# A decoder layer in one kernel: the first feed-forward's second products deferred and taken in chunks with seven block products

## The chip, the cores and the metric

The kernel runs on one core of one Trainium2 chip. The metric is the device time of one execution in microseconds. A core has five engines with their own instruction queues: TensorE (PE: matmuls, with weight loads shown apart as PEld), VectorE (DVE), ScalarE (ACT), GpSimd (POOL) and SyncE (SP), which here issues the transfers between DRAM and the on-chip memory SBUF. Matmuls write to PSUM, eight banks of 128 x 512 numbers in f32.

## The reference, cut to what matters

One decoder layer on x (1024 tokens, width 1024), all in f32. The two feed-forwards have a hidden width of 2816.

```python
mod = silu(cond) @ w_mod + b_mod        # nine vectors: shift, scale, gate for three sub-layers
h = modulate(rms_norm(x, ffn1_norm), sh1, sc1)
x = x + 0.5 * g1 * ((silu(h @ w_gate1) * (h @ w_up1)) @ w_down1)
h = modulate(rms_norm(x, mix_norm), sh2, sc2)
b, c, v, u = split(h @ w_in)
# group A: short gated convolution; group B: diagonal state space model (SSM) with a GLU
x = x + g2 * (concat(rms_norm(yA), rms_norm(yB)) @ w_out)
h = modulate(rms_norm(x, ffn2_norm), sh3, sc3)
x = x + 0.5 * g3 * ((silu(h @ w_gate2) * (h @ w_up2)) @ w_down2)
y = rms_norm(x, final_norm)
```

## The kernel before, in words

**Precision.** Each f32 product is made of three matmuls: every operand is split into a high and a low part (`hi` by a cast on ACT, `lo` by a subtraction on DVE), and `mm3` issues hi x hi, hi x lo and lo x hi, each 128 x 128 by 128 x 512, into one PSUM bank. Weights are split on the chip too: `Weights` loads arrays of 1 MB (`raw`), and `pump` turns them into "granules" (`w`, 128 x 1024, hi and lo), in a ring of three or four slots that come free as `ws.free()` is called.

**Layout.** x is held transposed in SBUF: eight tiles of 128 channels, each in two halves of 512 tokens (`x[k][h]`), from the start to the end. The left operands of a feed-forward (`act1`, `act3`) are eight tiles by two halves as well.

**Feed-forward.** The hidden width is cut into eleven groups of 256 (`NGRP`); `fa3` is group 3 of the first feed-forward, `fb3` of the second. A group has a first part (gate and up projections, `fa3g`, `fa3u`), an activation, and a second part (down projection, `fa3d`), which is added to x at once: 16 updates by DVE of the form x + gate * PSUM. A plain first part is 64 calls of `mm3`, a second part 32. `seven` makes a first part with seven products of 2 x 2 blocks in place of eight (Winograd's form): 56 calls, and in return sums and differences of blocks. Of the weights these are made by GpSimd in `combine` and `split_done` (`sums`, `raw`), of the activations by `combos` on DVE (S1 to S4), of the results by DVE between products. `SEVEN_FROM` = (6, 1): the first feed-forward has six plain groups and five of seven products, the second one and ten.

In the first feed-forward each group's second part follows its first part (`down_both`, `down2`; the last two are joined in `down`). In the second, groups 1 to 8 are handled otherwise: `seven` is given `kept`, so each group's activations and their block sums (seven left operands of 512 KB) are split and stored to DRAM; after group 10 `down7` takes two chunks of four groups (`fbd0`, `fbd1`), loads the left operands again (`fetch`) and makes the second parts with seven products, 112 calls of `mm3` a chunk; products 1, 3 and 5 add up in one PSUM bank, so each waits for the addition that has read it.

**Order.** The engines run in the order in which a scheduler at compile time puts the program; what the program sets is the priority. `mm3` ends with `clock.tick()`. `Clock` keeps a list of side work (generators), and every `period` ticks it takes one step of the first one. The side work of the first feed-forward is `side1`: `ssm_base` (small tables of the SSM), then for each of eight batches `ssm_batch` (matrices `cl`, `bl`, `rot` on DVE, small matmuls `kp`, `tp` on PE, stores to DRAM) with three `mod_block` each: vectors of `mod`, each one a product and sum over a 128 x 1024 tile of w_mod (`mod_vector`, in the trace the custom operation `wm`). `clock.period` is 2.75 in first parts and 8 in second parts of groups 1 to 4; before group 5 what is left of `side1` is issued at once, and `combos` follows with period 4. The gate g1 is made in the prologue, beside group 0's last products (`gate1`, eight `wm`), since group 0's second part needs it. `after1` starts the next norm's sum of squares once the last second part of a tile is added, and `norm_into` makes the mixer's left operand from it, 8 ticks, 7 ticks and one tick a tile later.

Pools that matter: `movs["A"]` (20 tiles of 4 KB a partition: left operands, `keep`), `movs["B"]` (12), `tmp` (6 tiles of 2 KB, `t2k`), six PSUM banks (`mm_ps`) for products.

Of the kernel before, what the change touches and what calls it, by code (L numbers as in the profile page):

```python
# [21 lines left out]
P = 128  # L22
# [12 lines left out]
SEVEN_FROM = (6, 1)  # L35

CHUNKS = (0, 2)
# [5 lines left out]
PAD = 96, 88  # L43
# [185 lines left out]
def hymba_layer(ctx: ExitStack, tc, x_d, wm1_d, wmod_d, gu1_d, gs1_d, wd1_d, win_d, wout_d, glu_d, gu2_d, gs2_d, wd2_d, ds2_d, cols_d, cond_d, lam_d, bc_d, out_d):  # L229
# [13 lines left out]
    xp = pool("xp", side="right")  # L243
# [41 lines left out]
    def stream(gu, gs, wd, ds, m):  # L285


        joined = m == 1
        first = NGRP - 2 - 4 * (0 if ds is None else ds.shape[0])
        for g in range(m):  # L290
            plain([gu[2 * g], gu[2 * g + 1]])
            if g < first and not (joined and g == m - 1):
                plain([wd[g]])
        for g in range(m, NGRP):
            j = len(srcs)
            inner = m - joined < g <= first
            srcs.extend([gs[g - m, 0], wd[g - 1], gs[g - m, 1]] if inner else [gs[g - m, 0], gs[g - m, 1]])
# [6 lines left out]
        for c in range(0 if ds is None else ds.shape[0]):  # L304
# [4 lines left out]
        j, n = len(srcs), wd.shape[0]  # L309
        srcs.extend([wd[n - 2], wd[n - 1]])  # L310
        granules.extend([(i, 2 * q), (i, 2 * q + 1)] for q in range(2) for i in (j, j + 1))

    stream(gu1_d, gs1_d, wd1_d, None, SEVEN_FROM[0])
    plain([win_d[i] for i in range(8)] + [glu_d] + [wout_d[i] for i in range(4)])
    stream(gu2_d, gs2_d, wd2_d, ds2_d, SEVEN_FROM[1])
# [3 lines left out]
    xt = [[xp.tile([P, 2, HALF], F32, tag=f"x{k}_{h}", name=f"x{k}_{h}") for h in range(2)] for k in range(KT // 2)]  # L319
    x = [[xt[k // 2][h][:, k % 2, :] for h in range(2)] for k in range(KT)]  # L320
    clock = Clock(4)

# [128 lines left out]
    def mod_fetch():  # L451
        if later:
            n, b = later.pop(0)
            pool_ = (raw1, raw2)[len(later) % 2]
            r = pool_.tile([P, 2, 1024], F32, tag="raw", name=f"wm{n}_{b}")
            SP.dma_start(r[:], wmod_d[n - 2, b])
            fetched.append((n, b, r))

    def mod_block():
        n, b, r = fetched.pop(0)  # L460
        s = sb.tile([P, 2], F32, tag="ms", name=f"ms{n}_{b}", bufs=2)
        for i in range(2):
            mod_vector(r[:, i, :], s[:, i : i + 1])
            yield
        mod_done(n, 2 * b, 2 * b + 2, s[:])
        mod_fetch()


    def gu_evac(fi, h, pg, pu, a_tiles, name):
# [3 lines left out]
        a_tiles[fi, h] = split_act(af[:], name + "a")  # L473

# [30 lines left out]
    def combos(act, name, homes, engine=None):  # L505
# [6 lines left out]
        G_ = engine or V  # L512
# [11 lines left out]
        while "free" not in blocks:  # L524
            yield
        for k in range(4):
            f12, s2 = whole(a12[k], f"f12_{k}", G_), whole(blocks["S2"][k], f"s2_{k}", G_)
            yield
            G_.tensor_tensor(out=f12[:], in0=f12[:], in1=s2[:], op=ALU.subtract)
            blocks["S4"].append(split_act(f12[:], f"{name}S4_{k}", homes[3]))  # L530
# [4 lines left out]
    def seven(name, between, place=1, kept=None, then=None):  # L535
# [3 lines left out]

        def keep(left, src):  # L540
            t = mov(f"{name}{left}")
            A.copy(t[:, 0, :], src[:])
            V.tensor_tensor(out=t[:, 1, :], in0=src[:], in1=t[:, 0, :].bitcast(F32), op=ALU.subtract)
            SP.dma_start(kept[left][:], t[:].bitcast(F32))

        def minus(dst, a, b):
            V.tensor_tensor(out=dst[:], in0=a[:], in1=b[:], op=ALU.subtract)
# [1037 lines left out]
```

## Time and profile before

| | |
|---|---|
| median of 3 runs | 1755.64 us (1754.24 to 1756.39) |
| profiled execution | 1754.16 us, its span 1752.0 us |
| TensorE clock granted, mean | 0.994 |
| busy: TensorE, VectorE, ScalarE, GpSimd | 1697.6, 1241.8, 527.9, 272.1 us |
| DMA | 227.96 MB, mean 130 GB/s |
| prologue and group 0 of the first feed-forward | to 86 us |
| rest of the first feed-forward | 86 to 755 us |
| mixer | 755 to 1084 us |
| second feed-forward | 1084 to 1752 us |

The profile is of one execution. Its span goes from the first to the last instruction. In its rows, L105 is the line of the helper that records most operations, so groups are told apart by the names of their tiles: out<-in, with buffer numbers left out. A row of the timeline gives start, duration, engine, line, operation, tiles and count, and in brackets the idle time of the engine before it and what ended that. A row of a stretch gives its length, then busy time and number of instructions of PE, PEld, DVE, ACT and POOL, then the granted clock, the DMA engines' busy share and the rate in GB/s.

### The profile page before, as it was taken

The page shows a single profiled execution, that of the slowest core. Times are in us where ns is not written, and L with a number is a line of the kernel's source. Part 1 is how long each engine was busy: PE and PEld are TensorE (multiplying, and loading weights), DVE is VectorE, ACT ScalarE, POOL GpSimd, SP SyncE. Part 2 cuts the span into 40 slices and gives each one's busy share as a digit, 9 for nine tenths or more (in the row PEclk, how much of TensorE's full clock was granted, in tenths as well). Part 3 has the DMA queues.
Part 4 walks back from the last instruction along what each step waited for, and adds up shares of the span by engine and source line. Part 5 has one row for each costly group of instructions (what it writes and reads, how often), then busy time and mean ns, then how long its engine had stood idle before and what let it go on. Part 6 is the DMA issues. An engine that isn't in the chain of part 4 may idle for free.

```text
span 1752.0 us, 20474 instructions
## 1 busy us (share of the span) xinstructions
PE 1697.6 (97%) x7676; PEld 1400.3 (80%) x7676; DVE 1241.8 (71%) x2249; ACT 527.9 (30%) x838; POOL 272.1 (16%) x193
## 2 busy tenths in 40 slices
PE   4999999999999999999899999999999999999996
PEld 3787888888888888878788888878888888888886
DVE  7999998985766555573566746987777667677656
ACT  4211212122223223242212523433344443322221
POOL 0000000001112122110000021023222323323311
PEclk9999999999999999999999999999999999999998
DMA  7533556521111112214664110013344334659312
GB/s 313 218 90 130 209 189 226 195 102 39 37 60 49 48 49 72 91 50 131 198 195 130 45 52 25 24 71 146 144 161 174 147 133 157 247 232 370 110 49 96
DMA packets 76020, 227.96 MB, mean 130 GB/s; under 512 B 16273, under 2 KB 31889, under 8 KB 61202
## 3 DMA queue, kind: packets, MB, share of 16 engines
q1 hardware_dynamic: 75922, 226.66, 36.6%
q8 instruction: 60, 0.98, 0.2%
q14 instruction: 38, 0.31, 0.1%
HBM read 172.10 MB, written 50.33 MB: 127 GB/s over the span
## 4 chain that ended last, share of the span: by engine, by line
PE 84%; DVE 10%; DMA 3%; ACT 1%; issue 1%; SPq 0%; POOL 0%; DVEq 0%; ACTq 0%; POOLq 0%
PE wo L105 5%; DVE w L105 2%; PE fb10d L105 2%; PE p L105 2%; PE u L105 2%; PE fa10d L105 2%; PE fbd_1B L105 2%; PE fbd_0B L105 2%; PE b L105 1%; DMA swz<-si 1%; PE fa4u L105 1%; PE fa3g L105 1%; PE fa2u L105 1%; PE fa3d L105 1%; PE fbd_1A L105 1%; PE fb0g L105 1%
## 5 line engine op out<-in xcount | busy, mean ns | idle before, releaser
L105 ACT CAST w<-raw 128x512 fp32r<-128x512 f32 (+1 forms) x310 | 220.7, 734 | 565.8 <-issue 78.4
L105 DVE TENSOR_TENSOR w<-raw,w 128x512 fp32r<-128x512 f32 (+1 forms) x310 | 276.3, 906 | 135.6 <-ACT w L105 133.9
L161 POOL TENSOR_TENSOR sums<-raw 128x512 f32<-128x512 f32 x38 | 53.3, 1403 | 546.8 <-PE fa5u L105 409.8
L170 POOL TENSOR_TENSOR raw<-sums,raw 128x512 f32<-128x512 f32 x38 | 57.0, 1500 | 377.8 <-DVE w L105 377.3
L172 POOL TENSOR_TENSOR raw<-raw 128x512 f32<-128x512 f32 x38 | 58.6, 1543 | 111.1 <-DVE w L105 111.1
L162 POOL TENSOR_TENSOR raw<-raw 128x512 f32<-128x512 f32 x38 | 58.5, 1540 | 3.0
L105 DVE CUSTOM_DVE_ANT_0 wm<-wm,cact 128x1024 f32<-128x1024 f32 x48 | 57.9, 1212 | 0.0
L105 PE MATMUL p<-h,w 128*128 128x512 f32 x192 | 49.3, 419 | 8.3 <-DVE h L105 5.4
L105 PEld LDWEIGHTS p<-h,w 128*128 128x128 f32 x192 | 38.9, 204 | 18.5 <-DVE h L105 6.7
L361 POOL TENSOR_TENSOR n3aq<-n3aq,n3aq 128x512 f32<-128x512 f32 x5 | 6.4, 1290 | 274.1 <-ACT n3aq L105 273.9
L105 DVE TENSOR_TENSOR w<-sums,w 128x512 fp32r<-128x512 f32 x38 | 46.9, 1242 | 1.2 <-ACT w L105 0.8
L105 PE MATMUL v<-h,w 128*128 128x512 f32 x192 | 46.9, 395 | 0.0
L105 PE MATMUL c<-h,w 128*128 128x512 f32 x192 | 46.6, 394 | 0.0
L105 PE MATMUL wo<-oa,w 128*128 128x512 f32 x192 | 45.4, 391 | 0.6 <-DVE w L105 0.6
L105 PE MATMUL u<-h,w 128*128 128x512 f32 x192 | 44.8, 392 | 0.8 <-DVE w L105 0.8
L105 PE MATMUL b<-h,w 128*128 128x512 f32 x192 | 45.6, 393 | 0.0
L105 PE MATMUL wo<-ob,w 128*128 128x512 f32 x192 | 45.2, 391 | 0.0
L105 PEld LDWEIGHTS u<-h,w 128*128 128x128 f32 x192 | 35.6, 188 | 9.1 <-DVE w L105 1.2
L105 PEld LDWEIGHTS wo<-oa,w 128*128 128x128 f32 x192 | 35.8, 188 | 8.7 <-DVE w L105 1.0
L105 PEld LDWEIGHTS wo<-ob,w 128*128 128x128 f32 x192 | 35.8, 188 | 7.4
L105 PEld LDWEIGHTS b<-h,w 128*128 128x128 f32 x192 | 35.5, 188 | 7.2
L105 PEld LDWEIGHTS c<-h,w 128*128 128x128 f32 x192 | 35.4, 188 | 7.0
(1361 smaller groups left out, 4004.8 us busy)
## 6 DMA issues: line engine op xcount, KB each, us to landing
raw<-in_gs SPq DMA_DIRECT2D x30, 1024.0 KB, 4.9
wm<-in_wmod SPq DMA_DIRECT2D x24, 1024.0 KB, 5.7
raw<-in_gu SPq DMA_DIRECT2D x14, 1024.0 KB, 5.6
raw<-in_wd SPq DMA_DIRECT2D x14, 1024.0 KB, 4.8
mw<-in_wm SPq DMA_DIRECT2D x8, 1024.0 KB, 12.5
raw<-in_win SPq DMA_DIRECT2D x8, 1024.0 KB, 5.8
raw<-in_ds SPq DMA_DIRECT2D x8, 1024.0 KB, 6.2
x<-in_x SPq DMA_DIRECT2D x8, 512.0 KB, 8.2
```

Of the source, the lines that this page charges most:

```text
L105: r = getattr(self.engine, name)(*args, **kw)
L161: self.G.tensor_tensor(out=f, in0=r[2], in1=r[1], op=ALU.subtract)
L162: self.G.tensor_tensor(out=r[1], in0=r[1], in1=r[0], op=ALU.subtract)
L170: self.G.tensor_tensor(out=r, in0=s["t3"], in1=r, op=ALU.add)
L172: self.G.tensor_tensor(out=r, in0=r, in1=s["t2"], op=ALU.subtract)
L361: nc.gpsimd.tensor_tensor(out=a, in0=a, in1=sq[:, :n], op=ALU.add)
```

## The change

- `SEVEN_FROM` becomes (4, 1): in the first feed-forward groups 4 to 10 are made with seven products.
- Second parts of the first feed-forward: groups 1 to 8 keep seven left operands each in DRAM and are made by `down7` in two chunks after group 10, as in the second feed-forward. Groups 0, 9 and 10 keep their four activations in DRAM too, and their second parts are joined in `last_parts`, which goes over the two halves of the output channels and within them over the two halves of the tokens.
- The plain groups get `gu_keep` in place of `gu_evac`: activations and their block sums are split and stored.
- x is given up after group 0's left operands are made (`xp_open.close()`), and its SBUF goes to other pools; before group 9 it is loaded again.
- Side work: g1 moves out of the prologue into the first SSM batches (`gate1`); `combos` runs between `ssm_base` and the batches; S4 is made by `combos_last`, put first in the list of side work at the last plain group; the other `mod` vectors become `side2`, a vector a step, from group 9 on. Periods: 4 in groups 1 to 3, 6.5 in groups 4 to 8, 6 from group 9 on (also beyond the first feed-forward).
- The ring of weight slots has three from group 1 on (`ring1` retired); `movs["B"]` opens before group 1.
- `combos_last` is used in the second feed-forward too, without the wait for group 0.

```diff
-SEVEN_FROM = (6, 1)
+SEVEN_FROM = (4, 1)
-CHUNKS = (0, 2)
+CHUNKS = 2
+LAST = ((0, NGRP - 2, NGRP - 1), (NGRP - 2, NGRP - 1))
...
+    def mod_tile(home):
+        n, d, r = fetched.popleft()
+        dst = (mods, scl, gate)[n % 3][:, n // 3]
+        mod_vector(r, dst[:, d : d + 1])
+        if d == KT - 1:
+            mod_done(n, 0, KT, dst)
+        mod_fetch(home)
...
+    def keep(kept, left, src, name):
+        if left in kept:
+            t = mov(f"{name}{left}")
+            A.copy(t[:, 0, :], src[:])
+            V.tensor_tensor(out=t[:, 1, :], in0=src[:], in1=t[:, 0, :].bitcast(F32), op=ALU.subtract)
+            SP.dma_start(kept[left][:], t[:].bitcast(F32))
+    def keep_sums(kept, a11, a21, a22, name):
+        V.tensor_tensor(out=a22[:], in0=a21[:], in1=a22[:], op=ALU.add)
+        keep(kept, "S1", a22, name)
+        V.tensor_tensor(out=a21[:], in0=a11[:], in1=a21[:], op=ALU.subtract)
+        keep(kept, "S3", a21, name)
+        V.tensor_tensor(out=a22[:], in0=a22[:], in1=a11[:], op=ALU.subtract)
+        keep(kept, "S2", a22, name)
+    def keep_last(kept, a12, s2, name):
+        V.tensor_tensor(out=a12[:], in0=a12[:], in1=s2[:], op=ALU.subtract)
+        keep(kept, "S4", a12, name)
+    def gu_keep(fi, h, pg, pu, afs, kept, name):
+        t = t2k(f"{name}{fi}_{h}")
+        A.activation(t[:], pg[:], AF.Silu)
+        V.tensor_tensor(out=t[:], in0=t[:], in1=pu[:], op=ALU.mult)
+        keep(kept, f"A{h + 1}{fi + 1}", t, name)
+        afs[fi, h] = t
+        if len(afs) == 4 and "S1" in kept:
+            keep_sums(kept, afs[0, 0], afs[0, 1], afs[1, 1], name)
+            keep_last(kept, afs[1, 0], afs[1, 1], name)
...
-        while "free" not in blocks:
+    def combos_last(act, name, home):
+        while "S3" not in blocks or len(blocks["S3"]) < 4:
             yield
         for k in range(4):
-            f12, s2 = whole(a12[k], f"f12_{k}", G_), whole(blocks["S2"][k], f"s2_{k}", G_)
+            f12, s2 = whole(act[0][4 + k], f"f12_{k}", V), whole(blocks["S2"][k], f"s2_{k}", V)
             yield
...
     def side1():
-        mod_fetch()
-        mod_fetch()
-        with tc.tile_pool(name="sb1", bufs=1) as sb1:
+        with tc.tile_pool(name="sb1", bufs=1, side="right") as sb1:
             yield from ssm_base(sb1)
...
+        for _ in range(2):
+            mod_fetch(mod_home)
+        yield from combos(act1, "h1", "BBB")
         for b in range(NB):
             yield from ssm_batch(b)
+    def side2():
+        for _ in range(2):
+            mod_fetch(mod_mov)
+        while fetched:
+            mod_tile(mod_mov)
+            yield
...
+    clock.side.append(side1())
+    clock.period = 4
+    for g in range(1, SEVEN_FROM[0]):
+        gate_up(act1, f"fa{g}", kept[g], g == SEVEN_FROM[0] - 1)
+    clock.period = 6.5
...
+    for g in range(SEVEN_FROM[0], NGRP):
+        if g == NGRP - 2:
             while clock.side:
                 clock.step()
+            side_open.close()
...
+            open_x(ctx)
+            for h in range(2):
+                load_x(h)
+            clock.period = 6
+            clock.side.append(side2())
+        seven(f"fa{g}", lambda: None, kept=kept[g], then=(lambda n: fetch_chunk(0, n)) if g == NGRP - 1 else None)
+    down7("fad0", lefts[0], 0, lambda n: fetch_chunk(1, n))
+    down7("fad1", lefts[1], 0, fetch_last)
...
+    def last_parts():
+        for dh in range(2):
+            wd = ws.take(3)
+            for h in range(2):
+                outs = [ps(f"fald{4 * dh + i}_{h}") for i in range(4)]
+                for q, (w, a) in enumerate(zip(wd, a_last)):
+                    for fi in range(2):
+                        for i, o in enumerate(outs):
+                            mm3(o[:], w, 4 * fi + i, a[fi, h], q == fi == 0, q == 2 and fi == 1)
+                    if h:
+                        ws.free()
+                for i, o in enumerate(outs):
+                    d = 4 * dh + i
+                    V.scalar_tensor_tensor(out=x[d][h], in0=o[:], scalar=gate[:, 0, d : d + 1], in1=x[d][h], op0=ALU.mult, op1=ALU.add)
+                    after1(d, h)
```

More of the change, by code (lines that the diff above doesn't have):

```diff
@@ L1164, in hymba_layer @@
+    last_parts()
+    while clock.side:
+        clock.step()
+    es1.close()
     ring1 = ring1_open.enter_context(tc.tile_pool(name="ring1b", bufs=1, side="right"))
@@ L1444, in group0 @@
         return a_tiles
[L1446 removed]
+    clock.side.extend([combos(act3, "h3", "BAA"), combos_last(act3, "h3", "A")])
     a_prev = group0()
[L1448 to L1449 removed]
+    kept = {g: kept_for(g, g not in LAST[1]) for g in range(1, NGRP - 1)}
     HOMES = dict(A11="B", S2="A", A12="B", S3="A", S1="B", A22="A", S4="A")
[L1451 removed]
+    lefts = [{left: [] for left in HOMES} for _ in range(CHUNKS)]
     a_last = {}
[L1454 to L1457 removed]
     def fetch_last(n):
```

275 lines of the change are left out of this document (120 added, 155 removed).

## The prediction

> **What bounds the kernel now.** I read the page first (busy times, chain), then the chain in order of time, TensorE's timeline, the stretches by stage, and last the groups of VectorE (DVE).
>
> ```profile
> span 1752.0 us, 20474 instructions
> PE 1697.6 (97%) x7676; PEld 1400.3 (80%) x7676; DVE 1241.8 (71%) x2249; ACT 527.9 (30%) x838; POOL 272.1 (16%) x193
> PE 84%; DVE 10%; DMA 3%; ACT 1%; issue 1%; SPq 0%; POOL 0%; DVEq 0%; ACTq 0%; POOLq 0%
> ...
> 410.99 10.88 PE fa5g L105 x48
> 465.39 2.72 PE fa6gC L105 x12
> ...
> 91.43 7.14 PE L105 MATMUL fa0d<-fa_0a,w 128*128 128x512 f32 x30 [0.65 <-ACT fa_0a L105]
> 163.90 5.81 PE L105 MATMUL fa1d<-fa_0a,w 128*128 128x512 f32 x18 [4.13 <-DVE x L105]
> ```
>
> TensorE is the chain, and it runs at one pace: 10.88/48 and 2.72/12 both give 0.2267 us a matmul, in plain groups and in seven-product groups. In the first feed-forward from 86 us on, TensorE waits in the two places shown: 0.65 + 4.13 = 4.78 us. So time there is matmuls times 0.2267, as long as VectorE keeps up. The stretches (busy us of PE, PEld, DVE, ACT, POOL, then clock, DMA share, GB/s) show how near it is to not doing so:
>
> ```profile
> 86.00:109.00 23.00, 22.34 (x97) 17.84 (x96) 22.55 (x41) 5.02 (x8) 0.00 (x0) 1.00 0.35 105
> 109.00:182.00 73.00, 68.87 (x302) 56.25 (x302) 69.55 (x338) 14.63 (x20) 0.00 (x0) 0.98 0.32 107
> 182.00:250.00 68.00, 68.00 (x311) 55.68 (x310) 65.20 (x125) 13.10 (x18) 0.00 (x0) 1.00 0.64 224
> 552.00:612.00 60.00, 60.00 (x266) 49.67 (x266) 36.20 (x50) 16.20 (x27) 11.71 (x8) 1.00 0.15 53
> 1192.00:1230.00 38.00, 38.00 (x169) 31.45 (x169) 27.13 (x40) 15.41 (x27) 11.41 (x8) 1.00 0.41 152
> 1536.00:1574.00 38.00, 38.00 (x170) 31.45 (x169) 26.37 (x31) 9.90 (x18) 13.13 (x8) 1.00 0.58 234
> ...
> 1130.00:1140.00 10.00, 9.00 (x38) 6.60 (x37) 10.00 (x17) 5.75 (x10) 0.00 (x0) 1.00 0.06 8
> 1140.00:1150.00 10.00, 9.24 (x38) 7.04 (x39) 10.00 (x17) 2.34 (x4) 4.98 (x2) 1.00 0.24 97
> 1150.00:1160.00 10.00, 10.00 (x46) 8.26 (x45) 10.00 (x17) 1.82 (x4) 2.29 (x1) 1.00 0.01 2
> ```
>
> In 182 to 250 VectorE is 96% busy beside plain groups with side work, and TensorE loses nothing. In 1192 to 1230 a seven-product group with its stores to DRAM leaves VectorE 11 us free. Only where VectorE is full (30 of 30 us from 1130 to 1160, side work beside a seven-product group) does TensorE lose 0.76 + 1.00 = 1.76 us.
>
> **The change, part by part.** *Matmuls.* A call of mm3 is three matmuls. First parts: before, six groups of 64 calls and five of 56, 664; after, four and seven, 648. Second parts: before 11 x 32 = 352; after two chunks of 112 and 3 x 32, 320. So 48 calls or 144 matmuls go: 144 x 0.2267 = **-32.6 us**, all on the path. The two waits shown belong to fa0d and fa1d, which no longer stand there; TensorE goes from group 0 straight to group 1, so **-4.8 us**. What is late next is VectorE's work, costed below. With no other loss the span is 1752.0 - 37.4 = 1714.6.
>
> *VectorE.* The rows it is costed from:
>
> ```profile
> L105 DVE SCALAR_TENSOR_TENSOR x<-fa7d,gate,x 128x512 f32<-128x512 f32 x16 | 12.0, 750 | 7.4 <-PE fa7d L105 7.3
> L105 DVE TENSOR_TENSOR fb1S<-fb1ut,fb1S 128x512 fp32r<-128x512 f32 x2 | 1.4, 684 | 0.0
> L105 DVE TENSOR_TENSOR w<-raw,w 128x1024 fp32r<-128x1024 f32 x43 | 52.4, 1219 | 18.5 <-ACT w L105 17.9
> L105 DVE TENSOR_TENSOR w<-sums,w 128x512 fp32r<-128x512 f32 x2 | 3.5, 1738 | 0.0
> L105 DVE CUSTOM_DVE_ANT_0 wm<-wm,cact 128x1024 f32<-128x1024 f32 x48 | 57.9, 1212 | 0.0
> L105 DVE TENSOR_TENSOR cl<-cl,clt 128x576 f32<-128x576 f32 x8 | 6.0, 750 | 0.0
> L105 DVE TENSOR_TENSOR bl<-bl,blt 128x512 f32<-128x512 f32 x8 | 5.5, 684 | 0.1
> L105 DVE TENSOR_TENSOR rot<-rot,rott 128x512 f32<-128x512 f32 x16 | 10.9, 681 | 0.1
> L105 DVE TENSOR_TENSOR bb<-prm,qr 128x64 f32<-128x64 f32 x16 | 3.4, 214 | 0.0
> ...
> 1194.79 0.69 DVE L105 TENSOR_TENSOR fb1S<-fb1ut,fb1S 128x512 fp32r<-128x512 f32 x1
> 1195.40 0.69 DVE L105 TENSOR_TENSOR fb1S<-fb1uu,fb1S 128x512 fp32r<-128x512 f32 x1
> ```
>
> In a full queue starts are 0.61 apart for 0.69 shown, so durations count at 0.88. It loses 160 - 48 = 112 updates of x (-75 us at 0.67) and gains 40 additions in down7, 24 splits, 32 differences and 20 additions in the two further seven-product groups (116 x 0.61 = +71) and 18 more weight granules (about 1.2 each, +22). As a total that is near even: some 18 us more in 32.6 us less. What matters is where it piles up, which I get from the planner: one side step every 4 calls in groups 1 to 3, 6.5 in groups 4 to 8, 6 after.
>
> Group 1 (43.5 us at pace): 16 of the 18 base steps of the SSM. All base steps are some 32 us, an estimate: VectorE's time from 86 to 182 (22.55 + 69.55) less 30 updates, 10 weights, 7 wm, 14 splits and products and three quarters of batch 0, by the rows. 28 + 4 weights (4.9) + 15 operations of keeping (9.2) + group 0's rest (2) = 44: full. Price between 0 (as in 182 to 250) and 4.78 x 43.5/96 = 2.2; I take 1. Groups 2 and 3 have 42 and 38 by the same count, no price.
>
> Groups 4 to 8: side1 has 18 + 12 + 48 yields and combos_last 8; by the end of group 3, 48 steps are gone, group 4 takes 8 or 9, so about 30 batch steps fall on three and a half groups, 8.6 a group. A batch after the gate vectors is 5 steps: three cl (2.26), three bl (2.05), six rot (4.09), six bb (1.3), two small (0.4) = 10.1, at 0.88 8.9 us, 1.78 a step. So VectorE needs 27.1 + 15.3 = 42.4 us, while TensorE needs 38.1 + 1.7 batches of kp and tp at 1.39 each (below), 40.5. That is 105%.
>
> ```profile
> 332.92 1.05 PE L105 MATMUL kp<-cl,bl 128*16 128x128 f32 x8
> 333.89 0.66 PE L105 MATMUL tp<-ident,bl 128*128 128x128 f32 x4
> 334.31 0.94 PE L105 MATMUL fa4u<-h,w 128*128 128x512 f32 x3
> ```
>
> Price: excess 1.9 x 3.5 = 6.6; or 1.76/30 of 138 us = 8.1. From below 0 (96% cost nothing in 182 to 250). I take **8.1**: the row with a seven-product group and a full VectorE is the nearest. Group 4 has S4 made late: its eight steps start 16 calls before, and the last is forced at the product that reads it: +1.
>
> Groups 9, 10 and down7: side2 has 48 vectors wm, one every 6 calls (4.08 us), 1.21 + 0.08. Groups 9 and 10 keep four left operands, not seven: 36.2 (552 to 612) less 16 updates and 2 weights, 23, + 12 = 35 of 38. Chunk 0: 26.4 + 12.1 = 38.5 of 38: full for 76 us. But there an accumulation waits for an addition that is three to four half products back (8 us), against 2.7 in a seven-product group; I take 2, between 0 and 4.5.
>
> *DMA and SP.* Added on SP's queue: 68 stores and 68 loads of 512 KB, 8 loads of x, and the vectors in 512 KB pieces. The stores wait in SP's queue for VectorE's splits, with weight loads behind them; the second feed-forward does the same 60 times and TensorE is at 38.00 of 38 there, so nothing. The loads of a chunk:
>
> ```profile
> 1530.00:1540.00 10.00, 10.00 (x46) 8.28 (x45) 9.59 (x12) 3.83 (x7) 4.86 (x4) 1.00 1.03 419
> ...
> fb1lS<-kept1S SPq DMA_DIRECT2D x4, 512.0 KB, 10.2
> wm<-in_wmod SPq DMA_DIRECT2D x24, 1024.0 KB, 5.7
> ```
>
> The queue is full there at 419 GB/s, and wm adds 128 GB/s (524288 B in 4.08 us). A product of chunk 1 is asked for when the same product of chunk 0 has ended its second pass and is read a pass later, 38.1 - 5.4 = 32.7 us, so that is covered; a wm in the middle is not (rival 3). [...]
>
> x is read again at group 9, some 90 us before its first update: nothing. The prologue loses 8 wm (they move into batches 0 to 2, inside the steps counted). At the end of the first feed-forward the first half's norm has 24 calls (16.3 us) to cover it, not 32; the only wait of u now is on a weight, so 0:
>
> ```profile
> 764.14 1.20 PE L105 MATMUL u<-h,w 128*128 128x512 f32 x4 [0.80 <-DVE w L105]
> ```
>  Period 6 stays for the second feed-forward, where combos runs at 4 now: fewer steps beside fb0d (at best its 1.76 us go), but four steps of S4 are forced at fb1 (two blocks of four operations and a cast, 2 x 5 x 0.61 = 6.1 us, less the 2.7 us of a product); +1, between -1.8 and +3.4.
>
> *Sum.* 1714.6 + 1 + 8.1 + 1 + 2 + 1 = 1727.7. The profiled execution took 1754.16, 2.16 more than its span, and the median of three runs is 1.48 above that: 1727.7 + 2.2 + 1.5 = **1731**.
>
> **The rivals.** (1) The cover holds: VectorE's work fits as in 182 to 250, and nothing is lost. 1714.6 + 3.6 = 1718. For it: the 96% of that stretch. Against: 105% in three groups.
>
> (2) VectorE against GpSimd. In 1192 to 1230 GpSimd is busy 11.41 us and the two w<-sums of VectorE take 1738 ns, not 684: it is held up, some 2.5 us a group now. 29 of the 39 operations of VectorE there read two SBUF tiles. If it is never idle, three quarters of 11.4, 8.5 us, collide: +6.0 a group, 48.4 against 40.5, 7.9 x 3.5 = 27.7 in place of 8.1: **1751**. Against: from 1130 to 1160 GpSimd ran 7.3 us beside a full VectorE and TensorE lost 1.76 in all. [...]
>
> (3) Slower: wm waits for its transfer. Two are in flight, so each has 8.16 us to land, and VectorE stands behind a wm that isn't there. Chunk loads land after 10.2. Were all 48 so late, a step takes 5.1, not 4.08: 48 x 1.0 = 49, less the 2 counted: 1778. It turns slower when the mean landing passes 9.2 us (24.2 us of gain left over 48 steps, 0.5 each). Against: the full stretches are some 70 of 196 us, and down7 has 8 us of cover.
>
> **How the numbers follow.** Forecast 0.54 (1722 to 1743), cover 0.23 (1716 to 1722), lock 0.14 (1743 to 1759), late wm 0.09 (above 1759). About 0.2% (3.5 us) is what can be told from no change: 1752.1 to 1759.2. Of the lock, 0.08 is below it, 0.06 in it. Faster 0.85, same 0.06, slower 0.09. 1717 to 1749 leaves out late wm, the upper half of the lock and the edge of the cover.
>
> **What would show it.** 7532 matmuls on TensorE; fa1g right after group 0, no fa0d before the chunks; idle of TensorE in groups 5 to 8 by DVE of about 8 us, VectorE at 95% there; the second feed-forward some 25 us earlier. Wrong if TensorE idles over 30 us there, or if VectorE idles for DMA wm.

## Result: slower by 2.2%

1794.22 us median (1793.23 to 1795.72) against 1754.94 (1753.06 to 1756.39): ratio 1.0225, 95% interval 1.0207 to 1.0243. Forecast were 1731 and, as the case on the other side, 1778.

The page of the changed kernel, its first part, the granted clock by slices, and the groups of the conversion of weights and of the vectors:

```profile
span 1792.4 us, 20836 instructions
PE 1690.4 (94%) x7532; PEld 1382.6 (77%) x7532; DVE 1307.8 (73%) x2286; ACT 569.0 (32%) x934; POOL 357.3 (20%) x241
...
PEclk9999999999999899999999999999999999999998
...
L107 ACT CAST w<-raw 128x512 fp32r<-128x512 f32 (+1 forms) x358 | 237.6, 689 | 564.3 <-POOL raw L172 139.3
L107 DVE CUSTOM_DVE_ANT_0 wm<-wm,cact 128x1024 f32<-128x1024 f32 x56 | 76.8, 1381 | 5.2 <-DMA wm<-in_wmod 5.1
```

The matmuls that were to go are gone (7532), and the span is still 40.4 us longer. All of it lies in the first feed-forward: from the end of group 0's first part to the first product of `u` it takes 710.4 us (from group 1's first product at 84.7 to 795.1), before 669.2 (from `fa0d` at 86.2 to 755.4). What follows takes 997.3 and 996.6. So the question is where in 710 us the saving went. From the starts of each stage's first product on TensorE, against the pace of the sum (0.2267 us a matmul, and 1.4 us for the `kp` and `tp` of a batch):

| stage | us | at pace | lost | allowed in the prediction |
|---|---|---|---|---|
| groups 1, 2 | 87.0 | 87.0 | 0 | 1 (with group 3) |
| group 3 | 53.8 | 46.3 | 7.5 | |
| groups 4 to 8 | 216.1 | 198.8 | 17.3 | 9.1 |
| groups 9, 10 | 80.6 | 76.2 | 4.4 | 2 (with the chunks) |
| two chunks (down7) | 205.6 | 152.3 | 53.3 | |
| last parts | 67.2 | 65.3 | 1.9 | 0 |

The view by windows (length, then busy time of PE, PEld, DVE, ACT and POOL, granted clock, DMA share and GB/s), for group 3, group 7, group 10, chunk 0, chunk 1 and the last parts:

```profile
171.80:225.60 53.80, 48.77 (x218) 39.34 (x217) 47.07 (x81) 13.97 (x23) 7.81 (x6) 0.94 0.62 196
...
353.00:401.40 48.40, 43.31 (x194) 34.53 (x192) 46.67 (x79) 17.83 (x31) 14.12 (x8) 0.96 0.46 164
...
477.40:522.30 44.90, 40.63 (x169) 32.15 (x168) 43.95 (x62) 13.72 (x24) 17.57 (x10) 0.96 0.73 252
522.30:637.90 115.60, 90.87 (x349) 68.20 (x349) 77.19 (x114) 18.95 (x34) 22.73 (x16) 0.90 0.90 337
637.90:727.90 90.00, 82.55 (x337) 64.83 (x336) 65.85 (x90) 19.21 (x33) 21.10 (x14) 0.94 0.72 265
727.90:795.10 67.20, 67.20 (x306) 55.87 (x305) 26.79 (x44) 16.69 (x23) 10.92 (x8) 1.00 0.14 48
```

In groups 7 and 10 VectorE is full (47 of 48 and 44 of 45 us), and in group 3 it is busy 47 of 54. In chunk 0 no engine is full: TensorE 79%, VectorE 67%, and only the DMA share is high (0.90, at 337 GB/s). So the two losses are of different kinds. What TensorE waits for, in the chunks and then in groups 3 to 8:

```profile
PE fad_0A L107 <- ACT w L107: 13.7, 2, 13.2
PE fad_0B L107 <- ACT w L107: 7.0, 4, 3.6
PE fad_0A L107 <- DVE w L107: 3.6, 2, 1.9
PE fad_0C L107 <- DMA fa1lS<-kept1S: 3.3, 2, 2.4
...
PE kp L107 <- DVE bl L107: 11.9, 5, 5.0
PE fa4gC L107 <- DVE fa4gt L107: 2.5, 1, 2.5
PE fa5gC L107 <- DVE fa5gt L107: 1.9, 1, 1.9
PE fa4gC L107 <- DVE h1S L107: 1.7, 1, 1.7
```

In the chunks it is the *weights* that are late, and most at one place, the second pass of chunk 0 (a chunk goes over its seven products twice, each pass for half of the output channels). The timeline there, of SyncE's queue (start, length of the run of issues, transfer, count), then VectorE, ScalarE and TensorE:

```profile
553.94 0.32 SPq L107 DMA_DIRECT2D kept10A<-fa10A  x1
...
565.72 0.32 SPq L107 DMA_DIRECT2D kept10A<-fa10A  x1
...
568.34 12.37 SPq L107 DMA_DIRECT2D wm<-in_wmod  x6
580.80 0.38 SPq L107 DMA_DIRECT2D raw<-in_ds  x1
582.26 0.33 SPq L107 DMA_DIRECT2D wm<-in_wmod  x1
582.68 1.11 SPq L107 DMA_DIRECT2D raw<-in_ds  x1
...
552.02 1.29 DVE L107 TENSOR_TENSOR w<-raw,w 128x512 fp32r<-128x512 f32 x2 [2.39 <-ACT w L107]
...
576.70 0.69 DVE L107 TENSOR_TENSOR fad_0u<-fad_0u,fad_0C 128x512 f32<-128x512 f32 x1 [4.44 <-PE fad_0C L107]
...
577.98 1.22 DVE L107 CUSTOM_DVE_ANT_0 wm<-wm,cact 128x1024 f32<-128x1024 f32 x1
...
589.82 0.62 ACT L107 CAST w<-raw 128x512 fp32r<-128x512 f32 x1 [36.28 <-DMA raw<-in_ds]
...
576.50 0.84 PE L107 MATMUL fad_1C<-fa4lS,w 128*128 128x512 f32 x3
590.49 2.04 PE L107 MATMUL fad_0A<-fa1lA,w 128*128 128x512 f32 x3 [13.15 <-ACT w L107]
```

VectorE ended the conversion of the first pass's weights at 553.3 (552.02 + 1.29), so the slots of `raw` were free from then on, and ScalarE idled 36.28 us. The loads that were to fill them were issued at 580.80 and 582.68, each right behind a `wm`. Ahead of them in the queue stood two stores of group 10, each waiting for VectorE's split, then fetches, then six `wm` that took 12.4 us to get out. Four of these left at once. The last two waited 8.9 us for a slot, which comes free when VectorE has run an earlier vector (SyncE's queue, 568 to 581):

```profile
SPq L107 <- DVE gate L107: 8.9, 2, 8.1
```

Those vectors, at 577.98, stand in VectorE's order behind additions that wait for TensorE's last products of the first pass. So the weights of the second pass could not be asked for before the first pass was all but over. TensorE was ready at 577.3 and got its weights at 590.5. It happens again, smaller, at each of the two later passes.

### The profile page after: what moved, and what is told of

Same layout as the page of the kernel before. It is cut to its first block, busy times and chain, and to the rows that moved or that the text cites. A ratio compares the mean times of both kernels' runs of the same rounds, so it can differ in the third digit from the quotient of the medians.

```text
span 1792.4 us, 20836 instructions
## 1 busy us (share of the span) xinstructions
PE 1690.4 (94%) x7532; PEld 1382.6 (77%) x7532; DVE 1307.8 (73%) x2286; ACT 569.0 (32%) x934; POOL 357.3 (20%) x241
## 3 DMA queue, kind: packets, MB, share of 16 engines
q1 hardware_dynamic: 100690, 302.17, 47.1%
## 4 chain that ended last, share of the span: by engine, by line
PE 59%; DVE 8%; DMA 5%; POOL 2%; issue 1%; ACT 1%; SPq 0%; DVEq 0%; POOLq 0%; ACTq 0%
PE wo L107 5%; PE fald L107 3%; PE fb10d L107 2%; DVE w L107 2%; PE u L107 2%; PE fbd_1B L107 2%; PE fbd_0B L107 2%; PE v L107 2%; PE b L107 1%; PE c L107 1%; PE fad_0B L107 1%; PE fad_1B L107 1%; PE fb0u L107 1%; PE fbd_1C L107 1%; PE fbd_0C L107 1%
## 5 line engine op out<-in xcount | busy, mean ns | idle before, releaser
L107 ACT CAST w<-raw 128x512 fp32r<-128x512 f32 (+1 forms) x358 | 237.6, 689 | 564.3 <-POOL raw L172 139.3
L107 DVE TENSOR_TENSOR w<-raw,w 128x512 fp32r<-128x512 f32 (+1 forms) x358 | 304.6, 868 | 141.1 <-ACT w L107 140.3
L172 POOL TENSOR_TENSOR raw<-sums,raw 128x512 f32<-128x512 f32 x50 | 81.3, 1626 | 448.1 <-DVE w L107 432.8
L163 POOL TENSOR_TENSOR sums<-raw 128x512 f32<-128x512 f32 x50 | 73.0, 1461 | 417.8 <-DMA raw<-in_gs 221.1
L174 POOL TENSOR_TENSOR raw<-raw 128x512 f32<-128x512 f32 x50 | 79.9, 1600 | 92.9 <-DVE w L107 89.5
L107 DVE CUSTOM_DVE_ANT_0 wm<-wm,cact 128x1024 f32<-128x1024 f32 x56 | 76.8, 1381 | 5.2 <-DMA wm<-in_wmod 5.1
L164 POOL TENSOR_TENSOR raw<-raw 128x512 f32<-128x512 f32 x50 | 79.8, 1595 | 3.9
L107 DVE TENSOR_TENSOR w<-sums,w 128x512 fp32r<-128x512 f32 x50 | 59.8, 1208 | 2.2 <-ACT w L107 1.9
L107 PE MATMUL u<-h,w 128*128 128x512 f32 x192 | 46.3, 401 | 0.2 <-DVE h L107 0.2
## 6 DMA issues: line engine op xcount, KB each, us to landing
mw<-in_wm SPq DMA_DIRECT2D x8, 1024.0 KB, 12.4
```

The costliest lines, as they stand in the source:

```text
L107: r = getattr(self.engine, name)(*args, **kw)
L163: self.G.tensor_tensor(out=f, in0=r[2], in1=r[1], op=ALU.subtract)
L164: self.G.tensor_tensor(out=r[1], in0=r[1], in1=r[0], op=ALU.subtract)
L172: self.G.tensor_tensor(out=r, in0=s["t3"], in1=r, op=ALU.add)
L174: self.G.tensor_tensor(out=r, in0=r, in1=s["t2"], op=ALU.subtract)
```

## The experiments

Stage times are read as above; "the chunks" are both, 205.6 us after the change. In the short diffs `+` and `-` are against the changed kernel.

**1. Is it the vectors, and what of them?** The chunks hold the deferred products and, as side work, some 29 of the 48 vectors `wm`. First all of them left out, then their transfers alone, then their bytes alone.

```
 def side2():
+    for n in (SC2, SH2, G2, SC3, SH3, G3):
+        V.memset(dst, 0.0); mod_done(n, 0, KT, dst); yield
```


> The 48 modulation vectors that the change put into groups 9 and 10 and the two deferred chunks are left out (their results are zero plus the bias), with their transfers and their vector work; all else is as after the change. Theories A (their 512 KB transfers stand in SyncE's in-order queue ahead of the deferred weights and the kept operands), B (their 24 MB fill the DMA engines) and C (their vector work delays VectorE) all expect the deferred chunks to fall from 205 us to 152 to 160 and the whole from 1794 to 1740 to 1750. The rival D, that the chunks' own loads (28 MB of kept operands and 8 MB of weights in 152 us) can't come in time whatever stands beside them, expects at most 10 us: 1784 or more.

1744.27 us, 0.9949 of before (0.9936 to 0.9963). The chunks took 157.4 (81.2 and 76.2), groups 9 and 10 78.3, the rest as after the change. So the kept operands and the deferred weights can come in time, and D falls: the chunks' 48 us belong to the vectors. It is also what the change is worth without this side work: 11.0 us (the kernel before, which does the 48 vectors, took 1755.28 beside it).

```
+    r = mod_mov("wm_zero"); V.memset(r, 0.0)
+    for d in range(KT): mod_vector(r, dst[:, d : d + 1]) ...   # no transfer
```


> The 48 vector operations stay where they are, but all on one resident tile of zeros; only their transfers are left out. A and B expect the same as without the vectors, 1740 to 1752. C expects no more than 5 us: 1789 or more. D: 1784 or more.

1765.14 us, ratio 1.0069 (1.0046 to 1.0091). The chunks stay at 159.4. But nothing holds the vectors back now: 28 of the 48 operations ran in groups 9 and 10, 20 in chunk 0 and none in chunk 1 (after the change 16, 19 and 11, the other two before group 9). So only chunk 0 compares like with like: 83.2 us beside 20 vectors, and 115.6 beside 19 with transfers. Groups 9 and 10 went from 78.3 to 94.9, with VectorE busy 91.0 of them. C is false for chunk 0 and right for those two groups.

```
-    SP.dma_start(r, wmod_d[n - 2, b, :, i, :])
+    SP.dma_start(r[:16], wmod_d[n - 2, b, :16, i, :])
```


> The 48 transfers and vector operations stay, with their places in SyncE's queue, their waits and their VectorE time, but each transfer and operation covers 16 partitions of 128, so each moves 64 KB instead of 512 KB (the other 112 partitions of the vectors' results are zero plus the bias). A, if it is the waiting for a slot at the head of the queue that costs, expects most of the 52 us to stay: 1780 to 1794. B, if it is the bytes, expects 1740 to 1755. C: 1789 or more. Between A and B (each about half) it would come out near 1768.

1792.89 us, 1.0230 (1.0207 to 1.0252): with an eighth of the bytes nothing is won (chunks 200.0). B is false as the main cause: the DMA share of 0.90 was not what held TensorE; bytes are worth 5.6 us there, and 3.9 with groups 9 and 10 counted in (82.3 us in that run).

**2. Is it SyncE's queue?** The transfers moved to another queue, moved later, and both.

```
-    SP.dma_start(r, wmod_d[...])
+    A.dma_start(r, wmod_d[...])
```


> As after the change, but the 48 vectors' transfers are issued by ScalarE's queue; their slots, bytes, vector work and time stay. If it is their wait at the head of SyncE's queue that holds up the deferred weights and kept operands (A), the two chunks fall from 206 us to 157 to 165, and groups 9 and 10, where the vector work is then no longer held back, take 80 to 95 us as without the transfers (95): the whole 1750 to 1765. The rival is that the same waits now hold up ScalarE's first halves of the weights, and nothing is won: 1785 to 1800.

1785.54 us, 1.0188 (1.0159 to 1.0218). The chunks fell to 176.0, so 30 of their 48 us go with the queue; groups 9 and 10 rose to 98.0, near the 94.9 without the transfers, and took 17 back: 12 us are won net. The whole misses the expectation by 20 us, 11 of them in the chunks and 3 in the two groups.

```
-        clock.side.append(side2())          # at group 9
+    clock.period = 6.5                      # before down7("fad0")
+    clock.side.append(side2())
```


> The 48 vectors begin with the first deferred chunk instead of group 9 and take one step each 6.5 products up to the end of the last parts; the queue is SyncE's as after the change. A, if each transfer in a chunk costs its share (48 us over some 30 transfers there, 1.6 us each), expects 34 of them in the chunks: chunks at 200 to 212 us, groups 9 and 10 at 78, the whole 1785 to 1800. If what costs is that the queue is already late when chunk 0 begins (the vectors in groups 9 and 10), the chunks fall to 160 to 175 us: 1748 to 1765.

1773.75 us, 1.0111 (1.0094 to 1.0129): chunks 187.6, groups 9 and 10 77.5. Between the two: with more vectors in the chunks (34) these lose less, 30 us instead of 48, so the vectors in groups 9 and 10, beside group 10's stores, had their share.

```
+    clock.side.append(side2())   # before down7("fad0"), period 6.5
-    SP.dma_start(r, wmod_d[...])
+    A.dma_start(r, wmod_d[...])
```


> Both: the vectors from the first chunk to the last parts, their transfers on ScalarE's queue. A expects the time without the vectors (1744) within a few us: 1743 to 1753, as their vector work showed no cost in the chunks (83 and 76 us with it). The rival of ScalarE's queue being held up: 1765 or more.

1767.83 us, 1.0079 (1.0062 to 1.0097); chunks 180.7. Not 1743 to 1753: ScalarE's queue is now held. In the view of waits of that run, ScalarE over the chunks and the last parts:

```profile
ACT w L107 <- DMA wm<-in_wmod: 29.0, 2, 19.6
```

The conversion of weights stood 29.0 us behind transfers of vectors. With thin transfers on that queue:

```
+    A.dma_start(r[:16], wmod_d[n - 2, b, :16, i, :])
```


> As the run with the vectors spread from the first chunk on and their transfers on ScalarE's queue (1768; chunks 181 us), but each transfer and vector operation covers 16 partitions of 128 (the rest of the results is zero plus the bias). If what is left of the chunks' loss there (181 against 157 us) is bytes, it goes: 1744 to 1752. If it is ScalarE's queue held at a slot, as the waits that SyncE's queue had, it stays: 1762 to 1770.

1761.73 us, 1.0043 (1.0028 to 1.0058), chunks 174.0: the queue held at a slot, as expected of that reading, and 6.7 us for the bytes, as in the other pair. Here a queue of its own didn't cure the wait (chunks 174.0, and 157.4 without the vectors); it only chose who stood behind it.

**3. The wait itself, or the slots it is for?** The vectors take their tiles from the pool of left operands: 20 slots, of which chunk 0 holds 16, and group 10's four stores and the vectors share the others.

```
+    mod_mov.slots = deque(mov(f"wms{i}") for i in range(4))   # go round four
```


> As the run with the vectors spread on SyncE's queue (1774; chunks 188 us), but the transfers go round four slots of their own, two of them on the way, so that each waits for the vector operation two steps back and not for the one just issued. If the wait at the head of the queue costs, the chunks fall by a third or more: 1752 to 1766. If it is the transfers as such: 1771 to 1777.

1775.19 us, 1.0117 (1.0101 to 1.0132), chunks 189.1, where the run that spread them had 187.6: no change. To wait for the vector two steps back was no better than for the last one; and the four are still four of the 20.

```
+    mod_mov.pool = tile_pool(name="wmq", ...)      # [P, 64], bufs=2
-    SP.dma_start(r, wmod_d[n - 2, b, :, i, :])
+    SP.dma_start(r[:, :64], wmod_d[n - 2, b, :, i, :64])
```


> As after the change, with the vectors in the same steps and on SyncE's queue, but in two slots of their own of 64 columns, so that they take none of the 20 slots of left operands; each transfer and vector operation covers 64 of 1024 columns (the results are sums over these alone). If the slots cost the 48 us (stores of group 10 and fetches wait for a slot, with the weights behind them in the queue), the chunks fall from 206 to 157 to 165 us: 1740 to 1756. If the vectors' own wait at the head of the queue costs, most of it stays: 1775 to 1794.

1754.81 us, 0.9993 (0.9982 to 1.0005), chunks 162.9: 43 of the 48 us gone with the vectors on the same queue, in the same steps. But the vector operation is short there too. With its time given back by a second operation of full length:

```
+    mod_vector(mod_mov.junk, pre[:, d : d + 1])
```


> As the run with slots of their own of 64 columns (1755; chunks 163 us), and besides each vector step has a second operation of full length (1.2 us) on one resident tile of zeros, so that VectorE has its full work back. If the slots are the cause, the chunks stay at 163 to 172 us and groups 9 and 10 take up to 16 us more, as they did with that work and no transfers: 1755 to 1775. If a full-length vector and its wait in the queue cost, as against the short one, the chunks are at 185 or more: 1778 or more.

1781.19 us, 1.0153 (1.0131 to 1.0176). The expectations are split: the chunks took 172.7, just past the upper end of what the slots expect and far from 185, while the whole lies in the range of the other reading (1778 or more), since groups 9 and 10 took 97.8. SyncE's queue at the second pass of chunk 0 in this run:

```profile
572.06 0.32 SPq L107 DMA_DIRECT2D kept10A<-fa10A  x1
...
574.22 0.99 SPq L107 DMA_DIRECT2D wm<-in_wmod  x2
575.31 0.62 SPq L107 DMA_DIRECT2D raw<-in_ds  x1
582.42 0.81 SPq L107 DMA_DIRECT2D wm<-in_wmod  x2
583.32 0.38 SPq L107 DMA_DIRECT2D raw<-in_ds  x1
```

Without the vectors, and then with their work but no transfers:

```profile
545.30 0.32 SPq L107 DMA_DIRECT2D kept10A<-fa10A  x1
...
547.48 1.05 SPq L107 DMA_DIRECT2D raw<-in_ds  x2
```
```profile
566.12 0.32 SPq L107 DMA_DIRECT2D kept10A<-fa10A  x1
...
568.31 1.03 SPq L107 DMA_DIRECT2D raw<-in_ds  x2
```

TensorE comes to chunk 0 at different times in these runs, so the rows are counted from the first product of group 9 (442.5 without the vectors, 445.0, 446.1, and 441.7 after the change), and groups 9 and 10 are added to the chunks:

| run | last store of group 10 | first weights of the second pass | groups 9 and 10 and chunks |
|---|---|---|---|
| no vectors | 102.8 | 105.0 | 235.7 |
| own slots, short operations | 102.8 | 106.0 | 241.1 |
| work alone, no transfers | 121.1 | 123.3 | 254.3 |
| own slots, full operations | 126.0 | 129.2 | 270.4 |
| shared slots, thin transfers | 121.5 | 137.7 | 282.3 |
| after the change | 124.0 | 139.1 | 286.3 |

The stores are late wherever VectorE has the vectors' full work, with transfers or without: it is that work, not the slots, that holds back the splits they wait for. What the shared slots add stands behind the last store. The weights follow it after 2 to 3 us in the other runs, and after 15 to 16 us with shared slots, where six `wm` in a row (12.37 us) stand between; with own slots two stand there (0.99), though the next two still waited 6.4 us for VectorE (the queue's gap from 576.0 to 582.42).

The converse, two slots held and no vectors:

```
+    hold = [mov(f"hold{i}") for i in range(2)]     # group 9 to the end of chunk 1
```


> As the run without the vectors (1744; chunks 157 us), but two of the 20 slots of left operands are held, unused, from group 9 to the end of the second chunk, as many as the vectors have on the way. No vector, transfer or wait of theirs is there. If the slots alone cost the 48 us, the chunks take 190 to 206 us: 1778 to 1794. If the slots cost only because a vector in the queue waits for one and everything behind it waits too, 1744 to 1760.

1748.07 us, 0.9960 (0.9948 to 0.9971), chunks 157.2, and 157.4 with those slots free. Slots alone cost nothing here. Of the 50.6 us that the vectors cost from group 9 to chunk 1, their work on VectorE alone costs 18.6, with the vectors where that run put them, and the transfers 32.0: 3.9 of these are bytes, and 11.9 or more go with slots of their own (the run with them has a second vector operation in each step, so more work on VectorE). How the remaining 16 divide between that extra work and waits in the queue is not settled; own slots for whole tiles, 8 KB a partition, were not tried.

**4. Groups 3 to 8.** First a step between `bl` and the matmuls that read it.

```
 yield from gate1()
+yield
 kp = sm(...)            # and clock.period 6.5 -> 6
```


> One more step of the clock between bl's last sum and the small matmuls that read it (kp, tp), as the modulation blocks gave before the change; period 6 for 6.5 from group 4 on, so that the side work still ends by group 8. If TensorE's idle time before kp (5.0 us in group 3, about 7 in groups 4 to 8) is owed to their following bl at once, it goes: 1780 to 1787. The rival, that VectorE is the bound there and the wait only changes its place (the accumulations' and the S4 waits grow by as much), expects 1792 to 1796.

1804.06 us, 1.0280 (1.0254 to 1.0305): slower still; groups 3 to 8 took 277.2, not 269.9. Group 3 stayed at 54.0, and the closer steps made 45.5 to 48.9 of groups 6 to 8. TensorE's waits at `kp` grew from 11.9 to 15.3 us. The step and the period were changed together, so neither is judged alone; the step did not take the wait away.

```
-    V.tensor_tensor(out=t[:, 1, :], in0=src, in1=t[:, 0, :], op=subtract)
+    A.copy(t[:, 1, :], src)
```


> As after the change, but the second halves of the kept operands of the first feed-forward are a copy by ScalarE instead of a difference by VectorE (the second halves are wrong by that): 7 operations of 0.68 us, 4.8 us a group, leave VectorE in groups 1 to 8. If VectorE's load costs groups 3 to 8 their 25 us, they fall from 270 us to 248 to 256, and the whole to 1772 to 1781. If it is the order of single waits (kp behind bl, the second part of bank C behind its addition) whatever the load, 1786 to 1794.

1779.84 us, 1.0140 (1.0124 to 1.0156): in the range for the load as a whole, not by the stages: 9.3 of the 14.4 us came in groups 9 and 10 and the chunks. The windows of groups 3 to 8, after the change and here:

```profile
171.80:441.70 269.90, 251.75 (x1130) 203.87 (x1129) 246.70 (x392) 99.47 (x172) 77.09 (x46) 0.98 0.50 174
```
```profile
172.60:435.80 263.20, 251.20 (x1130) 202.12 (x1129) 220.13 (x351) 119.26 (x214) 68.04 (x45) 0.99 0.49 176
```

VectorE is relieved of 26.6 us (246.7 to 220.1, 84% of the stretch) and 6.7 come back. Group 3 goes from 53.8 to 47.2, with 46.3 at pace, so *its* loss is VectorE's load. Groups 4 to 8 stay at 216.0: theirs isn't the load alone. The longest waits there are now, for VectorE and for ScalarE:

```profile
PE kp L107 <- DVE bl L107: 3.6, 2, 2.2
PE fa4gA L107 <- ACT fa4gt L107: 1.8, 1, 1.8
PE fa7uC L107 <- DVE fa7ut L107: 1.5, 1, 1.5
```

This run gave ScalarE 20 us of the work, so its waits are in part new; that leaves open how far a kernel with a free ScalarE would go.

Two more tried to relieve VectorE. The steps from group 5 on further apart, into group 9 (vectors as in the run that spread them on ScalarE's queue):

```
+if g == 5: clock.period = 8.5
-if g == NGRP - 2:               # side work ends, x comes back
+if g == NGRP - 1:
```


> As the run before, and besides x comes back at the start of group 10 instead of 9 and the state-space side work takes one step each 8.5 products from group 5 on instead of 6.5, so that group 9 bears a share of it. If groups 3 to 8 lose their 25 us to a VectorE that is full (its busy time there is 247 us where the products need 245), 5 to 12 us of it come back: 5 to 12 us below that run. The rival, that single waits in TensorE's order cost them and not the load, expects no change (2 us), and x's 4 MB beside chunk 0's fetches could cost 5 us.

1766.32 us against 1767.83: no gain. The sums of kept operands on GpSimd, on the run that follows:

```
-    V.tensor_tensor(out=a22, in0=a21, in1=a22, op=add)      # and three more
+    nc.gpsimd.tensor_tensor(...)                            # fa groups only
```


> As the run with the vectors in the last parts and the mixer, and besides the four sums of the kept operands (S1, S3, S2, S4) of each group of the first feed-forward go from VectorE to GpSimd. VectorE gets 2.7 us less in each of groups 1 to 8 (4 by 0.68), of a deficit that shows as 25 us in groups 3 to 8. If VectorE's load sets that loss, 8 to 15 us below that run. The rival, that GpSimd holds the temporaries too long or slows VectorE while it runs, expects 0 to 15 us above it.

1787.01 us, 22 above that run, more than its worst case of 15. Windows of groups 4 to 8 without and with the sums on GpSimd:

```profile
226.30:446.10 219.80, 206.17 (x914) 166.86 (x913) 199.39 (x311) 85.36 (x149) 68.90 (x40) 0.98 0.46 165
```
```profile
231.20:469.50 238.30, 214.52 (x914) 171.11 (x913) 198.24 (x296) 85.08 (x149) 90.90 (x58) 0.94 0.42 153
```

15 operations fewer, and VectorE is as busy (198.2 for 199.4, 10 less expected): those that are left got longer. GpSimd's own took up to 2.4 us where VectorE's take 0.68. So with more work on GpSimd VectorE's operations took longer: that was rival (2) of the prediction. It is at work in the changed kernel too. In its groups 5 to 8, two groups of operations of one shape, each with two SBUF operands (five of the first eight ran beside a GpSimd operation, and only two of the second five, in part):

```profile
L107 DVE TENSOR_TENSOR w<-sums,w 128x512 fp32r<-128x512 f32 x8 | 10.3, 1290 | 0.0
L107 DVE TENSOR_TENSOR bl<-bl,blt 128x512 f32<-128x512 f32 x5 | 3.4, 682 | 0.0
```

By the timeline, the 40 operations of this shape that overlap one of GpSimd and read no PSUM bank took 17.7 us more there than 0.68 us each, and the 121 that overlap none took 0.1 more; 17 that overlap one but read a PSUM bank took none. What TensorE would win without it was not tried.

**5. The vectors where there is room.** The 16 of the second norm in the last parts, 32 in the mixer:

```
+clock.period = 4;   clock.side.append(side2(mod_mov, (SC2, SH2)))            # last parts
+clock.period = 4.5; clock.side.append(side2(mod_mov, (G2, SC3, SH3, G3)))    # mixer
```


> The 48 vectors leave groups 9 and 10 and the deferred chunks: the 16 of the second norm go into the last parts (VectorE is 40% busy there, 27 of 67 us) at one each 4 products, the other 32 into the mixer's state-space stretch (VectorE 84 of 160 us busy) at one each 4.5, with three slots. Theory A and the run without the vectors (1744) expect 1743 to 1754. The rival, that their waits at the head of SyncE's queue now hold up the mixer's own loads, expects 1760 or more.

1764.98 us, 1.0060 (1.0043 to 1.0078). The chunks took 157.2, 48 us less, and the mixer lost 19 of that: 346.6 us from `u` to the second feed-forward, not 327.5, as the rival expected. TensorE waits there for SyncE's loads:

```profile
PE px L107 <- DMA ub<-u_d: 6.0, 4, 2.6
PE px L107 <- DMA si<-si_d: 4.1, 1, 4.1
```

Then 24 and 24, the mixer's on ScalarE's queue:

```
+clock.period = 4; clock.side.append(side2(mod_mov, (SC2, SH2, G2)))          # last parts
+clock.period = 6; clock.side.append(side2(mod_mov, (SC3, SH3, G3)))          # mixer
+(A if n in (SC3, SH3, G3) else SP).dma_start(r, wmod_d[...])
```


> The vectors of the second norm and its gate (24) go into the last parts, one each 4 products; the other 24 into the mixer, one each 6, with their transfers on ScalarE's queue, so that the mixer's loads on SyncE's queue have none in front of them. The run with 16 and 32, all on SyncE's queue, had the chunks at 157 us and lost 19 us in the mixer. If that was SyncE's queue again: 1744 to 1752. If it is VectorE's chain through the state-space steps, 1755 to 1765.

1783.86 us, 1.0162 (1.0146 to 1.0178): worse than both expectations. Eight `wm` stood 20 us in ScalarE's queue ahead of a copy, and the state-space stretch stood behind them:

```profile
818.07 20.10 ACTq L107 DMA_DIRECT2D wms<-in_wmod  x8
...
846.55 2.07 PE L107 MATMUL px<-ub,mi 128*128 128x128 f32 x8 [27.74 <-DMA ub<-u_d]
```

The first gate's vectors out of groups 3 to 5 as well:

```
 for b in range(NB): yield from ssm_batch(b)      # without gate1
+while fetched: mod_tile(mod_home); yield         # clock.period 9 from group 5, 6 from 9
```


> As the run before, and besides the 8 vectors of the first gate (9.8 us of VectorE) leave the batches of groups 3 to 5 for groups 8 and 9, and the steps from group 5 on come each 9 products. x comes back at group 10. If VectorE's load costs groups 3 to 8, 4 to 10 us below that run; if not, within 2 us of it.

1785.98 us, 1.0176 (1.0158 to 1.0194): 2.1 us above the run before, at the bound for "not the load"; groups 3 to 8 took 278.2. No version with all of its vectors beat the kernel before.

## Why the prediction was wrong

- **The saving**: the count was right, 7532 matmuls with `fa1g` at 84.7 behind group 0. But even without the 48 vectors the kernel is only 11.0 us faster than before, where some 24 were forecast with them.
- **"The stores wait in SP's queue for VectorE's splits, with weight loads behind them; ... so nothing"**: this is the step that failed, and with it the 2 us (0 to 4.5) for the vectors in down7 with groups 9 and 10, which lost 57.7 (7.2 of it also without the vectors). The second feed-forward does it at pace, but no vector stands in its queue or in VectorE's order. Here the vectors' work made the splits late, and with them the stores and the weights behind them (18.6 us by the run without transfers); and their transfers stood between the stores and the weights, waiting for slots that VectorE frees (the other 32.0, bytes 3.9 of them). Without the vectors the weights of the next pass were asked for 11.4 us before TensorE read them (547.48 and 558.84) and came just in time (a wait of 0.34 us), so there was no slack: here they came 13 us late. The prediction's counts of VectorE's work were near (77.2 us in chunk 0, where 77 were counted); it counted each queue's bytes and its issues, not what each entry waits for.
- **Rival 3** had the place and the size (1778 for 1794) and the wrong mechanism: VectorE waited for a `wm` 5.1 us in all, the mean landing was not what decided, and an eighth of the bytes gave 1.3 us back in the whole. Its chance of 0.09 rested on "8 us of cover" and on bandwidth; 419 GB/s said nothing of what an entry in the queue waits for.
- **Rival 2** (the lock of the chances) was at work at about half of its size: 17.7 us in groups 5 to 8 are 4.4 a group, where it had 8.5 for a VectorE that is never idle. That three quarters collide was the author's estimate, from the 29 of 39 operations with two SBUF tiles; in groups 5 to 8 it is 40 operations without a PSUM bank that took the 17.7 us, and 17 with one took nothing more. Whether TensorE lost by it is open.
- **Groups 4 to 8**: 9.1 allowed, 17.3 lost; why the waits there stay when VectorE has less to do is open. VectorE is 95% busy in groups 5 to 8, as predicted (164.9 of 173.3 us), and TensorE's waits for it there are 9.1 us, near the 8 predicted; but they cost 12.6 us of time (see the last section). In group 4 the late S4 and bank C took 4.7 where 1 was given. **Group 3** had no price, by a count of 38 us of VectorE's work; it was busy 47.1, and 7.5 us were lost. That count was too low.
- **x, the norm tail, the second feed-forward**: right. From `u` on 0.7 us longer, +1 predicted.

The excess over the terms is 55.7 + 8.2 + 6.5 + 1.9 = 72.3 us; 1792.4 less the predicted span of 1727.7 is 64.7. Most of the difference is in where the sum began: its 1714.6 had 5.9 us above pace from before (631.8 for the 625.9 at pace), which the stage table counts as lost, and group 1 starts 1.5 earlier.

## What to carry over

Before side work with transfers goes into a stage, write down the order of the queue there and, for each entry, what it waits for, through to the engine that frees its slot. Here transfers that waited 8.9 us for their slots held up the weights behind them, and with an eighth of the bytes the chunks still took 200.0 us, not 205.6. Set against such a wait the slack of the most urgent load behind it: the weights of the second pass had none even without the vectors, and here TensorE waited 13.15 us for them. Do the same for the engine that does the side work: the splits behind the vectors made the stores late with no transfer in the way (18.6 us from group 9 to chunk 1). To divide such a loss, leave out the work, the transfers and the bytes one at a time, and add up all the stages among which the loss can move; the chunks alone would have given the slots 27 us, with groups 9 and 10 it is 12. A stage that runs at pace elsewhere is a proof only with the same entries in the queue.

## What the runs showed of the hardware

In these runs some waits of TensorE cost more than their length. In the run with slower side steps, 2.71 us of waiting in group 6 is followed by twelve matmuls in 4.55 us where the twelve before it took 2.88, with a granted clock of 0.66 from 329 to 334 us:

```profile
323.47 2.88 PE L107 MATMUL fa6gE<-h,w 128*128 128x512 f32 x12
329.07 4.55 PE L107 MATMUL fa6gC<-h1S,w 128*128 128x512 f32 x12 [2.71 <-DVE fa6gt L107]
```

After the 13.15 us in chunk 0 three matmuls take 2.04 us, and 0.84 before it; the granted clock is 0.54 in the idle slice and still 0.78 in the next:

```profile
580.00:590.00 10.00, 0.00 (x0) 0.00 (x0) 6.42 (x13) 0.18 (x1) 0.14 (x1) 0.54 0.87 310
590.00:600.00 10.00, 8.73 (x26) 5.88 (x27) 7.72 (x8) 2.62 (x5) 7.72 (x5) 0.78 0.95 357
```

Not every wait did. In groups 3 to 8 of the changed kernel the eight `kp` took 1.03 us behind a wait of 1.63, and 1.75 and 1.86 behind waits of 3.18 and 5.03; twelve matmuls behind a wait of 1.86 took 2.97, near the 2.88 elsewhere:

```profile
207.78 1.86 PE L107 MATMUL kp<-cl,bl 128*16 128x128 f32 x8 [5.03 <-DVE bl L107]
...
288.31 2.97 PE L107 MATMUL fa5gC<-h1S,w 128*128 128x512 f32 x12 [1.86 <-DVE fa5gt L107]
...
368.38 1.03 PE L107 MATMUL kp<-cl,bl 128*16 128x128 f32 x8 [1.63 <-DVE bl L107]
...
392.87 1.75 PE L107 MATMUL kp<-cl,bl 128*16 128x128 f32 x8 [3.18 <-DVE bl L107]
```

So the waits of 18 us in groups 3 to 8 (269.9 less 251.75 busy) go with a loss of 25. The wait of 2.71 cost 1.67 more (4.55 less 2.88). What sets the size of such a loss was not shown.
